# Merge gates as a stage of their own, and a recurrent state carried by a diagonal product, in a hybrid RWKV-7 and RG-LRU layer

## The chip, the cores and the metric

One Trainium2 chip, one of its cores. The metric is device microseconds of one execution; a median over runs is given where a kernel ran several times.

## The reference

One layer over 512 latent tokens behind 256 context tokens, D_MODEL 1024, fp32: half a SwiGLU FFN, two token mixers side by side on one normalised input (RWKV-7 with 16 heads of 64 in both directions, and an RG-LRU), merge gates, one output projection, and another half FFN. Cut to what this change touches:

```python
def rwkv_step(s, inp):
    r, w, k, v, kk, kka = inp
    sa = jnp.einsum('bhvk,bhk->bhv', s, -kk)
    s = s * w[:, :, None, :] + sa[..., None] * kka[:, :, None, :] + v[..., None] * k[:, :, None, :]
    y = jnp.einsum('bhvk,bhk->bhv', s, r)
    return s, y
```

The gates are two further column blocks of the input projection, 1024 columns each; a sigmoid of one scales the RWKV branch's projection, a sigmoid of the other the RG-LRU's, and the two are added.

## The kernel before

Features lie on the partitions. An fp32 product runs as three products of split operands (hi with hi, hi with lo, lo with hi: `dense`, L197 to L199), so 128 output features of 512 tokens are a column of 24 matmuls. A weight arrives by a DMA on SP's queue (L170) and is split by two instructions, hi (L161) and lo (L179), on ACT and DVE in the FFNs and on POOL in most of the input projection.

The stages are: the first FFN (to about 640 us); the input projection, eight units j of 128 features each; the recurrent stage `rwkv_phase`; the merge, the output projection and the second FFN (from about 2027 us). In the input projection each unit makes its keys, the RG-LRU's gates, then `merge_gates(j)` (two columns, a tanh on ACT, and a DMA to grw_d and glru_d), decays, reads, values and the scans; nearly all that the next stage needs goes through DRAM.

The recurrent stage has 16 units, eight pairs of heads by two directions, of 12 chunks of 64 tokens. Per unit it

- loads bk, ar and pc (`loads`), and makes the chunk Gram matrices (`gram`, 64x64 products, masks on ACT and DVE);
- inverts the triangular ones (`invert`: 31 steps of two DVE instructions, L830 and L832) and brings the result back through two DMAs, with a merge of the blocks on TensorE (`merge`, L870 and L884);
- transposes values and decays keys on TensorE (`fetch`), the latter by a diagonal matrix dg = eye * pc that POOL makes;
- walks through the 12 positions (`chain`). A position has the hops right (w = products of values and of the state s), solve (u = Y w) and step (the new state). w and u are copied out of PSUM by ACT (L941). The new state is s * pc plus two products, vt with bt and u with bt, by one DVE instruction (L984); the first state is a memset (L949).

One iteration is 24 hops, six positions of each of two units, whose chains are interleaved with a half-unit's offset: unit i is in its second half while unit i + 1 is in its first. The right side, u and the state's sum of one chain lie in one PSUM bank, ch0 or ch1 by direction.

The order of all this is written by hand: `iteration(i)` puts each operation at a hop (the table WIN), and the program is emitted in that order on all engines. Between the chain's hops lie the gram of unit i + 3, the inversion (DVE), the merge and fetch of unit i + 2, the layer norm of a finished pair (`finish`) and pieces of the filler: the RG-LRU's projection w_plru, 128 pieces of three matmuls (L1084 to L1086) whose inputs are ylru tiles (split at L202 and L203) and whose weights POOL and ACT split. In the prologue of this stage 48 pieces stand before and after the inversion of unit 0; unit 1 is inverted and merged in iteration -1, beside the first half of unit 0's chain.

Of the kernel before, what the change touches and what calls it, by code (L numbers as in the profile page):

```python
# [56 lines left out]
def hybrid_layer_kernel(ctx: ExitStack, tc, xT, vecs, cst_in, w_mod, wg1, wu1, wd1, w_in, w_up, a_up, g_up,  # L57
# [80 lines left out]
    def open_hn(st, n):  # L138
        p = st.enter_context(tc.tile_pool(name=f"hn{n}", bufs=1, reuse_waits="tile"))
# [292 lines left out]
    def input_phase():  # L432
        with ExitStack() as st:
# [257 lines left out]
            for j in range(KT):  # L691
# [4 lines left out]
                merge_gates(j)  # L696
# [15 lines left out]
    def rwkv_phase(outer):  # L712
        with ExitStack() as st:
            open_psum(st, "ps_rwkv")
            rp = outer.enter_context(tc.tile_pool(name="rwkv", bufs=1, reuse_waits="tile"))
            units = ExitStack()
            up = units.enter_context(tc.tile_pool(name="units", bufs=1, reuse_waits="tile"))
            work = lambda: bank("wk", 3)
# [13 lines left out]
            def t768(tag, bufs):  # L732
                return up.tile([128, NT], F32, tag=tag, name=tag, bufs=bufs)

            def t512(tag, bufs):
                return rp.tile([128, XT], F32, tag=tag, name=tag, bufs=bufs)
# [156 lines left out]
            def fetch(i):  # L893
                u = us[i]

                def decays():
                    j, d = divmod(i, 2)
                    u["v"] = t768("vs", 2)
                    nc.sync.dma_start(out=u["v"], in_=(zv_d, zvr_d)[d][j])
                    u["dg"] = up.tile([128, NCH, C], F32, tag="dg", name="dg", bufs=1)  # L900
                    G.tensor_tensor(out=u["dg"], in0=eye2.unsqueeze(1).to_broadcast([128, NCH, C]),
                                    in1=u["pc"].unsqueeze(2).to_broadcast([128, NCH, C]), op=ALU.mult)
                    u["bt"] = up.tile([128, NCH, 2, C], F32, tag="bt", name="bt", bufs=3)
                    u["vt"] = up.tile([128, NCH, C], F32, tag="vt", name="vt", bufs=3)
# [22 lines left out]
            def chain(i):  # L927
# [8 lines left out]
                def state():  # L936
                    return up.tile([128, C], F32, tag=f"s{d}", name="s", bufs=2)

# [63 lines left out]
            def finish(j):  # L1002
# [13 lines left out]
                def var():  # L1016
# [4 lines left out]
                    m = rp.tile([128, 12], F32, tag="rqm", name="rqm", bufs=1)[:, :8]  # L1021
                    V.tensor_scalar(out=m, in0=acc[:, :8], scalar1=1.0 / 64, scalar2=LN_EPS, op0=ALU.mult, op1=ALU.add)
                    r = rsqrt(m, 8, rp)
# [21 lines left out]
            def filler():  # L1045
# [3 lines left out]
                HX = XT // 2  # L1049

                def raw(src, c, p):
                    def go():
                        t = x["raw", c, p] = rp.tile([128, 512], F32, tag="fraw", name="fraw", bufs=2)
# [122 lines left out]
            def prologue():  # L1176
                def now(ops):
                    for op in ops:
                        op()
# [205 lines left out]
```

## Time and profile before

| | |
|---|---|
| median of 3 runs | 2550.93 us (2542.09 to 2554.51) |
| profiled execution | 2539.91 us, span 2538.1 us |
| TensorE's matmuls, busy | 2178.6 us, 86% of the span |
| VectorE | 1331.0 us, 52% |
| ScalarE | 879.5 us, 35% |
| GpSimd | 384.5 us, 15% |
[...]
| chain that ended last | PE 36%, DVE 13%, DMA 9%, issue 3%, ACT 3% |

A matmul's end is modelled, and one may overlap the next, so the distance between starts tells more than the duration. An idle time is put down to what ended it. PE is TensorE, DVE VectorE, ACT ScalarE, POOL GpSimd and SP the engine whose queue issues the DMAs.

### The profile page before, as it was taken

The numbers are of one execution on the slowest core, as the hardware profiler recorded it, in microseconds if no ns is written. First come the engines' busy times: TensorE is split into PE (matmuls) and PEld (weight loads), VectorE is DVE, ScalarE is ACT, GpSimd is POOL, SyncE is SP. The second block draws the span as 40 slices with busy tenths as digits, with TensorE's granted clock in tenths as the row PEclk, the third lists the DMA queues.
The fourth block names the chain that finished last, engine by engine and source line by source line (L and its number), as shares of the span: only waits on it lengthen the run. The fifth ranks groups of instructions, "written<-read, shape, count | busy, mean of one in ns | idle before, by whom it ended". The sixth has DMA issues, their size and how long they took to land.

```text
span 2538.1 us, 48576 instructions
## 1 busy us (share of the span) xinstructions
PE 2178.6 (86%) x19840; PEld 1832.7 (72%) x19840; DVE 1331.0 (52%) x2955; ACT 879.5 (35%) x1769; POOL 384.5 (15%) x336
## 2 busy tenths in 40 slices
PE   5999999999797989979853687578878799999997
PEld 3787878788686768767643677567777578888886
DVE  5332232235864867757654565467776356333335
ACT  5222212224554556445541232233333234322223
POOL 1000000000643434434311110011111000000000
PEclk8999999999898989989977688699999789999999
DMA  7515241223336564456663443335543352233233
GB/s 279 195 54 187 65 168 63 88 71 100 123 84 123 132 130 107 106 128 134 117 134 95 102 118 94 92 82 125 131 111 77 118 173 91 86 106 92 89 93 92
DMA packets 254655, 289.06 MB, mean 114 GB/s; under 512 B 153952, under 2 KB 172640, under 8 KB 250208
## 3 DMA queue, kind: packets, MB, share of 16 engines
q1 hardware_dynamic: 252128, 283.34, 41.2%
q10 hardware_dynamic: 2304, 2.62, 0.6%
q8 instruction: 155, 2.54, 0.4%
q14 instruction: 68, 0.56, 0.1%
HBM read 229.96 MB, written 55.93 MB: 113 GB/s over the span
## 4 chain that ended last, share of the span: by engine, by line
PE 36%; DVE 13%; DMA 9%; issue 3%; ACT 3%; SPq 1%; POOL 0%; ACTq 0%; DVEq 0%; POOLq 0%
PE mm L197 8%; PE mm L198 7%; PE mm L199 7%; PE wk L760 5%; PE ch L760 4%; DVE pr L830 2%; DMA ga_d<-sh 2%; DVE yl L832 2%; DMA y<-yt 2%; PE y L966 1%; DMA ar<-ar_d 1%; DVE s L984 1%; SPq L854 1%; PE wk L870 1%; DMA graw<-in_lru_wx_dram 1%
## 5 line engine op out<-in xcount | busy, mean ns | idle before, releaser
L197 PE MATMUL mm<-hnh,whi 128*128 128x512 f32 (+1 forms) x1896 | 672.2, 356 | 27.3 <-ACT gr L475 20.3
L198 PE MATMUL mm<-hnl,whi 128*128 128x512 f32 (+1 forms) x1896 | 670.4, 354 | 2.5 <-POOL hnl L203 1.8
L199 PE MATMUL mm<-hnh,wlo 128*128 128x512 f32 (+1 forms) x1896 | 666.9, 352 | 0.0
L197 PEld LDWEIGHTS mm<-hnh,whi 128*128 128x128 f32 x1896 | 365.3, 193 | 94.1 <-issue 38.2
L198 PEld LDWEIGHTS mm<-hnl,whi 128*128 128x128 f32 x1896 | 365.7, 193 | 58.6 <-issue 7.4
L199 PEld LDWEIGHTS mm<-hnh,wlo 128*128 128x128 f32 x1896 | 365.3, 193 | 48.0
L161 ACT ACTIVATE whi<-wraw 128x512 fp32r<-128x512 f32 (+3 forms) x264 | 193.9, 736 | 594.2 <-PE mm L198 492.5
L179 DVE TENSOR_TENSOR wlo<-wraw,whi 128x512 fp32r<-128x512 f32 (+3 forms) x264 | 216.1, 819 | 302.5 <-ACT whi L161 298.9
L197 PE MATMUL mm<-hh,whi 128*128 128x256 f32 (+1 forms) x592 | 201.4, 341 | 0.4 <-ACT hh L202 0.4
L198 PE MATMUL mm<-hl,whi 128*128 128x256 f32 (+1 forms) x592 | 201.1, 340 | 0.3 <-DVE hl L203 0.3
L199 PE MATMUL mm<-hh,wlo 128*128 128x256 f32 (+1 forms) x592 | 201.0, 340 | 0.0
L179 POOL TENSOR_TENSOR wlo<-wraw,whi 128x512 fp32r<-128x512 f32 x118 | 173.7, 1478 | 6.2
L161 POOL CAST whi<-wraw 128x512 fp32r<-128x512 f32 x118 | 101.3, 859 | 330.8 <-PE mm L198 254.9
L319 DVE TENSOR_TENSOR hf<-mm,sl 128x256 f32<-128x256 f32 (+1 forms) x68 | 40.1, 590 | 211.9 <-PE mm L199 210.0
L830 DVE TENSOR_TENSOR pr<-yl,wl 96x126 f32<-96x126 f32 (+22 forms) x496 | 140.6, 283 | 16.3 <-DMA wl<-nd 5.2
L203 POOL TENSOR_TENSOR hnl<-nt,hnh 128x256 fp32r<-128x256 f32 (+1 forms) x28 | 27.3, 976 | 796.3 <-ACT hnh L202 649.0
L832 DVE TENSOR_TENSOR yl<-yl,pr 96x126 f32<-96x126 f32 (+22 forms) x496 | 137.5, 277 | 17.1
L760 PE MATMUL wk<-ar,bk 64*64 64x128 f32 (+1 forms) x1536 | 103.7, 292 | 32.6 <-DMA ar<-ar_d 30.1
L197 PEld LDWEIGHTS mm<-hh,whi 128*128 128x128 f32 x592 | 113.0, 191 | 15.4 <-issue 1.7
L199 PEld LDWEIGHTS mm<-hh,wlo 128*128 128x128 f32 x592 | 112.9, 191 | 15.5 <-issue 2.5
L198 PEld LDWEIGHTS mm<-hl,whi 128*128 128x128 f32 x592 | 112.9, 191 | 14.3 <-issue 0.8
L760 PEld LDWEIGHTS wk<-ar,bk 64*64 64x64 f32 x1536 | 90.0, 164 | 38.8 <-issue 36.1
(239 smaller groups left out, 3414.8 us busy)
## 6 DMA issues: line engine op xcount, KB each, us to landing
wm<-in_w_mod_dram SPq DMA_DIRECT2D x32, 1024.0 KB
wraw<-in_w_in_dram SPq DMA_DIRECT2D x118, 256.0 KB
wraw<-in_wd_dram SPq DMA_DIRECT2D x64, 256.0 KB
bk_d<-bk SPq DMA_DIRECT2D x16, 768.0 KB
bk<-bk_d SPq DMA_DIRECT2D x15, 768.0 KB
wraw<-in_wg_dram SPq DMA_DIRECT2D x44, 256.0 KB
wraw<-in_wu_dram SPq DMA_DIRECT2D x44, 256.0 KB
wraw<-in_wg_dram SPq DMA_DIRECT2D x22, 512.0 KB
```

Of the source, the lines that this page charges most:

```text
L161: self.copy = (lambda o, i: eng.tensor_copy(o, i)) if eng else (lambda o, i: S.activation(o, i, AF.Copy))
L179: self.sub.tensor_tensor(out=l[:, :m], in0=raw[:, :m], in1=h[:, :m], op=ALU.subtract)
L197: PE.matmul(acc, lhsT=wh, rhs=xh, start=k == 0, stop=False)
L198: PE.matmul(acc, lhsT=wh, rhs=xl, start=False, stop=False)
L199: cur["pe"] = PE.matmul(acc, lhsT=wl, rhs=xh, start=False, stop=k == n - 1).ins.name
L203: eng.tensor_tensor(out=lo, in0=src, in1=hi, op=ALU.subtract)
L319: V.tensor_tensor(out=hf[:, :n], in0=pu[:, :n], in1=sl[:, :n], op=ALU.mult)
L760: PE.matmul(out[hp[h]], lhsT=lhsT[hp[h]], rhs=rhs[hp[h]], start=start, stop=stop)
L830: V.tensor_tensor(out=pr[:, :ni, :nt], in0=yl[:, :ni, t:t + 1].to_broadcast([96, ni, nt]), in1=wl[:, t:t + 1, t + 1:].to_broadcast([96, ni ...
L832: V.tensor_tensor(out=yl[:, :ni, t + 1:], in0=yl[:, :ni, t + 1:], in1=pr[:, :ni, :nt], op=ALU.subtract)
L854: nc.sync.dma_start(out=Y[p0:p0 + 32, :, 32 * b:32 * b + 32], in_=yd[m0:m0 + 12].rearrange("m s t -> s m t"))
L870: PE.matmul(acc[hi:hi + 32, 32 * c:32 * c + 32], lhsT=u["n"][lo:lo + 32, c, 32:64], rhs=u["y1"][lo:lo + 32, c, :].rearrange("p (q i) -> p ...
```

## The change

1. `merge_gates` leaves the input projection. Its 16 columns become `gate_columns`, the prologue of the recurrent stage: the columns follow one another on TensorE, the two grams and merges of units 0 and 1 stand between them, and both inversions are put beside them on DVE. The weights are split by ACT and DVE instead of POOL; the accumulators are the banks ch0 and ch1.
2. The pools of the normalised input and of its weights stay open until then, on the right side of SBUF, and what the chains fetch is opened in their place afterwards (vs has one buffer, was two; dg three, was one).
3. The state is no longer made by DVE: the pair dg with s is added in PSUM to the two other products, and ACT copies the sum. The products vt with bt and dg with s are issued in `solve`, behind the copy of u. The first position has no product with the state, and no memset.
4. All 128 pieces of the filler lie in the iterations: 6 in each of iterations -1 to 12 (before, 5 or fewer), some 15 in each of the last three; its ylru tiles are loaded four ahead, and those of the second half are split one after each piece of the first half's last block.

```diff
-            def merge_gates(j):
-                for col, dst in ((COL_MRW + j, grw_d), (COL_MLRU + j, glru_d)):
-                    w = wp.load(w_in[col], KT)
-                    acc = mm()
-                    dense(acc, w, hn_pairs(CT, XT))
-                    sg = t512("sg", 1)
-                    table(sg, acc, AF.Tanh, scale=0.5)
-                    nc.sync.dma_start(out=dst[j], in_=sg)
...
                 def right(pos):
                     def go():
                         c = seq[pos]
-                        if pos == 0:
-                            u["s"] = state()
-                            V.memset(u["s"], 0.0)
                         chb = u["chb"] = bank(f"ch{d}", 1)
-                        each_head(chb[:, 0:C], u["gm"][:, c], u["vt"][:, c], stop=False)
-                        each_head(chb[:, 0:C], a_of(u, c), u["s"], start=False)
+                        each_head(chb[:, 0:C], u["gm"][:, c], u["vt"][:, c], stop=pos == 0)
+                        if pos:
+                            each_head(chb[:, 0:C], a_of(u, c), u["s"], start=False)
                         u["w"] = copied(chb[:, 0:C], "w")
...
                 def solve(pos):
                     def go():
+                        c = seq[pos]
                         acc = u["chb"][:, 2 * C:3 * C]
-                        each_head(acc, u["Y"][:, seq[pos]], u["w"])
+                        each_head(acc, u["Y"][:, c], u["w"])
                         u["u"] = copied(acc, "u")
+                        if pos < last:
+                            acc = u["chb"][:, C:2 * C]
+                            each_head(acc, u["bt"][:, c, 1], u["vt"][:, c], stop=False)
+                            if pos:
+                                each_head(acc, u["dg"][:, c], u["s"], start=False, stop=False)
...
                 def step(pos):
...
-                            each_head(acc, u["bt"][:, c, 1], u["vt"][:, c], stop=False)
                             each_head(acc, u["bt"][:, c, 0], u["u"], start=False)
-                            nxt = state()
-                            V.scalar_tensor_tensor(out=nxt, in0=u["s"], scalar=u["pc"][:, c:c + 1], in1=acc, op0=ALU.mult, op1=ALU.add)
-                            u["s"] = nxt
+                            u["s"] = copied(acc, "s")
...
+                def load(n):
+                    if n < 2 * KT:
+                        q, k = divmod(n, KT)
+                        x["y", n] = rp.tile([128, HX], F32, tag="fr", name="fr", bufs=4)
+                        nc.sync.dma_start(out=x["y", n], in_=ylru_d[k, :, HX * q:HX * q + HX])
+                def mixed(n):
...
+                    split(*x["a", n], x.pop(("y", n)))
+                    load(n + 4)
...
+                        if q == 0 and m == KT - 1:
+                            mixed(KT + k)
...
+            def gate_columns():
...
+                def part(n):
+                    if n < len(cols):
+                        x["w", n] = []
+                        for t in x.pop(("raw", n)):
+                            h, l = [wpool.tile([128, 512], F32R, tag=f"w{w}", name=f"w{w}", bufs=WB[1]) for w in ("hi", "lo")]
+                            split(h, l, t)
+                            x["w", n].append((h, l))
+                def column(n):
...
+                        part(n + 1)
+                        load(n + 2)
+                        w = x.pop(("w", n))
+                        acc = bank(("ch0", "ch1")[n % 2], 1)
+                        dense(acc, lambda k: [t[:, 128 * (k % 4):128 * (k % 4) + 128] for t in w[k // 4]], hn_pairs(CT, XT))
+                        sg = wpool.tile([128, XT], F32, tag="sg", name="sg", bufs=1)
+                        S.activation(sg, acc, AF.Tanh, scale=0.5)
+                        nc.sync.dma_start(out=cols[n][1], in_=sg)
...
+                for i in range(3):
+                    beside(0, 1, loads(i))
+                first(0, 1)
+                first(1, 3)
+                inverse(0, 3, 8)
+                inverse(1, 8, 13)
+                beside(9, 10, [lambda: [op() for op in merge(0)]])
+                beside(14, 15, [lambda: [op() for op in merge(1)]])
```

What moves is seen in the order of the instructions. First TensorE at two positions of the interleaved chains, before: the solves (w with Y, here ybd) of both chains stand one behind the other, then the products of the state. A number behind ch or ybd tells one buffer from another, a bracket the engine whose instruction a row waits for.

```order
L760 MATMUL ch_15537<-w,ybd_10913 64x64 [waits Activation_49]
L760 MATMUL ch_15537<-w,ybd_10913 64x64
L760 MATMUL ch_15544<-w,ybd_10917 64x64 [waits Activation_49]
L760 MATMUL ch_15544<-w,ybd_10917 64x64
L760 MATMUL ch_15537<-vt,bt 64x64 [waits Activation_49]
L760 MATMUL ch_15537<-vt,bt 64x64
L760 MATMUL ch_15537<-u,bt 64x64 x2
L760 MATMUL ch_15544<-vt,bt 64x64 [waits Activation_49]
L760 MATMUL ch_15544<-vt,bt 64x64
L760 MATMUL ch_15544<-u,bt 64x64 x2
L988 MATMUL y<-gm,u 64x64 x2
L760 MATMUL wk<-dg,bk 64x64 x16
```

The same place after the change:

```order
L756 MATMUL ch_12053<-w,ybd_10268 64x64 [waits Activation_49]
L756 MATMUL ch_12053<-w,ybd_10268 64x64
L756 MATMUL ch_12053<-vt,bt 64x64 [waits Activation_49]
L756 MATMUL ch_12053<-vt,bt 64x64
L756 MATMUL ch_12053<-s,dg 64x64 x2
L756 MATMUL ch_12060<-w,ybd_10270 64x64 x2
L756 MATMUL ch_12060<-vt,bt 64x64 [waits Activation_49]
L756 MATMUL ch_12060<-vt,bt 64x64
L756 MATMUL ch_12060<-s,dg 64x64 x2
L756 MATMUL ch_12053<-u,bt 64x64 x2
L982 MATMUL y<-gm,u 64x64 x2
L756 MATMUL ch_12060<-u,bt 64x64 x2
```

The products vt with bt (and the new s with dg) have moved up to stand between the two solves, and the first of each pair waits for ACT, where u is copied; the second chain's solve stands behind it.

Second, SP's queue at the end of the input projection, before: the last RG-LRU result ylru_d is followed by the loads of units 0 to 2 (bk and ar of unit 0 are on ACT's queue here), the Gram matrices' way through DRAM (nd, wl), and then values and filler.

```order
L683 DMA ylru_d<-gr 128x512
L751 DMA pc<-pc_d 128x12
L745 DMA bk<-bk_d 128x1536
L747 DMA ar<-ar_d 128x1280
L751 DMA pc<-pc_d 128x12
L745 DMA bk<-bk_d 128x1536
L747 DMA ar<-ar_d 128x1280
L751 DMA pc<-pc_d 128x12
L810 DMA nd<-gm 32x12x32 x4
L814 DMA wl<-nd 48x1024 x2
L899 DMA vs<-zv_d 128x768
L1071 DMA fr<-ylru_d 128x256 x8
```

And after the change:

```order
L673 DMA ylru_d<-gr 128x512
L1135 DMA grw_d<-sg 128x512
L741 DMA bk<-bk_d 128x1536
L743 DMA ar<-ar_d 128x1280
L747 DMA pc<-pc_d 128x12
L741 DMA bk<-bk_d 128x1536
L743 DMA ar<-ar_d 128x1280
L747 DMA pc<-pc_d 128x12
L741 DMA bk<-bk_d 128x1536
L743 DMA ar<-ar_d 128x1280
L747 DMA pc<-pc_d 128x12
L1112 DMA wraw<-in_w_in_dram 128x512 x2
```

The first gate's result (grw_d) stands ahead of the loads of units 0 to 2, all of which are on SP now, and the weights of a further column behind them.

## Rows read from the trace of the kernel before

**Rows 1.** Stages: length; busy of PE, PEld, DVE, ACT, POOL; clock; DMA share, GB/s.

```profile
728.00:1318.00 590.00, 504.76 (x2391) 402.49 (x2389) 396.77 (x547) 303.86 (x464) 234.11 (x201) 0.91 0.57 117
1318.00:1407.00 89.00, 33.53 (x432) 31.53 (x432) 29.30 (x88) 13.44 (x28) 13.49 (x11) 0.71 0.46 136
1407.00:1458.00 51.00, 36.44 (x628) 32.79 (x628) 33.70 (x118) 12.87 (x33) 9.55 (x8) 0.70 0.38 100
1458.00:1949.00 491.00, 377.99 (x8918) 345.25 (x8918) 320.72 (x1161) 144.86 (x504) 54.96 (x43) 0.89 0.43 105
```

**Rows 2.** TensorE's waits, 680 to 1310 us: total, times, longest.

```profile
PE mm L199 <- DVE glo L179: 29.2, 5, 10.4
```

**Rows 3.** TensorE's waits, 1420 to 2010 us.

```profile
PE ch L760 <- DVE s L984: 65.7, 45, 15.0
PE wk L870 <- DMA y<-yt: 26.6, 11, 3.6
PE ch L760 <- DVE s L949: 18.4, 14, 2.2
PE ch L760 <- ACT u L941: 18.2, 37, 1.2
```

**Rows 4.** Timeline of DVE, then of PE, prologue: start, duration, what, [idle before, releaser].

```profile
1317.74 0.69 DVE L682 TENSOR_TENSOR gr<-gr,gel 128x512 f32<-128x512 f32 x1
...
1422.38 0.28 DVE L984 SCALAR_TENSOR_TENSOR s<-s,pc,ch 128x64 f32<-128x64 f32 x1 [1.39 <-PE ch L760]
...
1327.94 8.79 PE L760 MATMUL wk<-ar,bk 64*64 64x64 f32 x160 [30.11 <-DMA ar<-ar_d]
...
1348.39 1.12 PE L760 MATMUL wk<-eye,vs 64*64 64x64 f32 x16 [7.17 <-DMA vs<-zv_d]
```

**Rows 5.** Timeline of all engines, one position of the last chain.

```profile
2002.10 0.33 PE L760 MATMUL ch<-w,ybd 64*64 64x64 f32 x4 [0.15 <-ACT w L941]
2002.54 0.22 ACT L941 ACTIVATE u<-ch 128x64 f32<-128x64 f32 x1 [0.49 <-PE ch L760]
...
2002.82 0.33 PE L760 MATMUL ch<-vt,bt 64*64 64x64 f32 x4 [0.38 <-ACT u L941]
...
2003.37 0.28 DVE L984 SCALAR_TENSOR_TENSOR s<-s,pc,ch 128x64 f32<-128x64 f32 x1 [2.15 <-PE ch L760]
...
2003.70 0.33 PE L760 MATMUL ch<-vt,gm 64*64 64x64 f32 x4 [0.32 <-DVE s L984]
```

**Rows 6.** Timeline of SP's queue, gates of unit 0.

```profile
728.34 0.33 SPq L626 DMA_DIRECT2D grw_d<-sg  x1
...
733.83 0.33 SPq L626 DMA_DIRECT2D glru_d<-sg  x1
```

**Rows 7.** The page's costliest groups: DVE's weight remainders.

```profile
L179 DVE TENSOR_TENSOR wlo<-wraw,whi 128x512 fp32r<-128x512 f32 (+3 forms) x264 | 216.1, 819 | 302.5 <-ACT whi L161 298.9
```

**Rows 8.** Timeline of PE at 1840 us, both levels of the clock.

```profile
1840.37 0.42 PE L966 MATMUL y<-gm,vt 64*64 64x64 f32 x4
1840.58 0.42 PE L966 MATMUL y<-ar,s 64*64 64x64 f32 x4
...
1843.53 0.28 PE L1084 MATMUL fl<-fx,fhi 128*128 128x256 f32 x1
1843.64 0.28 PE L1085 MATMUL fl<-fx,fhi 128*128 128x256 f32 x1
...
1844.37 0.28 PE L760 MATMUL ch<-vt,bt 64*64 64x64 f32 x4
1844.49 0.28 PE L760 MATMUL ch<-u,bt 64*64 64x64 f32 x4
```

**Rows 9.** Timeline of PE at the two long stalls.

```profile
1593.37 0.48 PE L760 MATMUL ch<-vt,gm 64*64 64x64 f32 x4 [11.90 <-DVE s L984]
...
1644.97 0.48 PE L760 MATMUL ch<-vt,gm 64*64 64x64 f32 x4 [15.03 <-DVE s L984]
```

More of the change, by code (lines that the diff above doesn't have):

```diff
@@ L1076, in piece, with raw @@
-                def piece(c, k, src, dst):
-                    def go():
+                rp = late["rp"]
+                flat = [(q, m, p) for q in range(2) for m in range(KT) for p in range(2)]
+                def raw(n):
+                    if n < len(flat):
+                        q, m, p = flat[n]
+                        t = x["raw", n] = rp.tile([128, 512], F32, tag="fraw", name="fraw", bufs=2)
+                        nc.sync.dma_start(out=t, in_=w_plru[m][:, 512 * p:512 * p + 512])
@@ new lines, in mixed, with piece @@
+                def mixed(n):
+                    k = n % KT
+                    x["a", n] = [rp.tile([128, HX], F32R, tag=f"fx{w}{k}", name=f"fx{w}{k}", bufs=1) for w in range(2)]
+                    split(*x["a", n], x.pop(("y", n)))
+                    load(n + 4)
+                def piece(n, k):
+                    def go():
+                        q, m, p = flat[n]
+                        if k == 0 and n == 0:
+                            raw(0)
+                            for y in range(4):
+                                load(y)
+                            raw(1)
+                            weights(0)
+                            for y in range(KT):
+                                mixed(y)
+                        if k == 4 * p:
+                            raw(n + 2)
+                            weights(n + 1)
@@ L1111, in filler, with load, go @@
-                return ops
+                return [piece(n, k) for n, (q, m, p) in enumerate(flat) for k in range(4 * p, 4 * p + 4)]
+            def gate_columns():
+                cols = [(COL_MRW + j, grw_d[j]) for j in range(KT)] + [(COL_MLRU + j, glru_d[j]) for j in range(KT)]
+                x = {}
+                def load(n):
+                    if n < len(cols):
+                        x["raw", n] = [wpool.tile([128, 512], F32, tag="wraw", name="wraw", bufs=WB[0]) for _ in range(2)]
+                        for p, t in enumerate(x["raw", n]):
+                            nc.sync.dma_start(out=t, in_=w_in[cols[n][0]][:, 512 * p:512 * p + 512])
+                def part(n):
+                    if n < len(cols):
+                        x["w", n] = []
[4 more added lines that the diff above has]
+                def column(n):
+                    def go():
+                        if n == 0:
+                            load(0)
+                            part(0)
+                            load(1)
+                        part(n + 1)
[6 more added lines that the diff above has]
+                        nc.sync.dma_start(out=cols[n][1], in_=sg)
+                    return go
+                return [column(n) for n in range(len(cols))]
@@ L1176, in prologue @@
             def prologue():
-                def now(ops):
-                    for op in ops:
-                        op()
-                def feed(n):
-                    now(fill[:n])
-                    del fill[:n]
-                for i in range(3):
-                    now(loads(i, nc.sync if i else nc.scalar))
-                for i in range(2):
-                    ops, out = gram(i)
-                    now(ops)
-                    out(QS[i])
-                now(fetch(0))
-                feed(PRO[0])
@@ L1193, in prologue, with beside, first @@
-                ops, back = invert(0)
-                now(ops)
-                back()
-                feed(PRO[1])
-                now(merge(0))
-                put(-1, [(-0.9, unit_invert(1, HOPS + 17.0, (HOPS, HOPS + 15.0)))])
+                gate = gate_columns()
+                todo = {n: [op] for n, op in enumerate(gate)}
+                def beside(a, b, ops):
+                    for at, op in spread(ops, a, b):
+                        todo[int(at)].append(op)
+                def first(i, at):
+                    ops, out = gram(i)
+                    beside(at, at + 1, ops[:3] + [out])
+                    beside(at + 1, at + 2, ops[3:])
@@ new lines, in inverse, with go @@
+                def inverse(i, a, b):
+                    def go():
+                        ops, back = invert(i)
+                        for op in ops[:n]:
+                            op()
+                        rest[i] = ops[n:], back
+                    n = 2
+                    rest = {}
+                    beside(a, a + 1, [go])
+                    for q in range(a + 1, b):
+                        def go(q=q):
+                            ops, back = rest[i]
+                            k = -(-len(ops) // (b - q))
+                            for op in ops[:k]:
+                                op()
+                            rest[i] = ops[k:], back
+                            if q == b - 1:
+                                back()
+                        beside(q, q + 1, [go])
```

113 lines of the change are left out of this document (41 added, 72 removed).

## The prediction

> **What bounds the kernel now.** I read the table by stage first. In the input projection TensorE works 504.8 us of 590, and in the recurrent stage 378.0 of 491 at a granted clock of 0.89; only in the prologue between them (89 us) is it busy for 33.5 us, at 0.71 [rows 1]. So TensorE is the engine to price, and an edit is worth what it does to TensorE's own work or to its idle time. The waits of TensorE come next: the longest of the input projection is on DVE's weight remainder, 29.2 us in 5 places [rows 2]; in the recurrent stage it waits for the state of DVE (65.7 us, 45 times), for a transposed inverse on its way through a DMA (26.6, 11), for the copy of u (18.2, 37) and for the memset of a state (18.4, 14) [rows 3]. Last I read single positions of the chain and the first chain step on the timeline [rows 4, 5].
>
> **The change part by part.** The sum is made against the profiled execution, 2539.9 us. That one is 0.4% below the median of the runs shown (2550.9), so what I forecast is the median plus the sum.
>
> *Gates out of the input projection.* The two results of a unit leave 5.49 us apart (728.34 and 733.83) [rows 6], which is one column of 24 matmuls. Sixteen of them are 88 us. Against that, the first two columns of the new stage have their four weight remainders on DVE inside the last unit, 0.82 us each [rows 7], 3 us. I take -85. The other bound: DVE and ACT follow TensorE closely in that stage (DVE 396.8 us of 590 [rows 1]) and the 29.2 us wait for DVE [rows 2] shows that TensorE can be held by it; were half of the gates' time only cover for DVE, -45 would be left. I choose the upper end because TensorE's idle time there, 85 of 590, is small beside the work. The weight splits that POOL did go with the gates, and POOL is busy 234 of 590 us [rows 1]: it gates nothing, so nothing is gained there.
>
> *Prologue.* Before, the last DVE instruction of the input projection starts at 1317.74 and the first state at 1422.38: 104.6 us, 30.1 of them TensorE's wait for ar [rows 4]. After, the queue order puts ar's load where it was, about 10 us behind that DVE instruction; two columns run before it lands, in time that is idle now, and 14 come behind it: 77 us. Two grams (most of their matmuls are one run of 8.8 us at the low clock [rows 4], so 11 for the two) and two merges, by estimate 6, stand between the columns. The inversions of units 0 and 1, DVE work, lie beside the columns, and the cover holds: a column needs 1.6 us of DVE for its two remainders [rows 7] and leaves 4 of its 5.5. With 7 us of hand-overs the columns end some 111 us after that mark. Then vs is loaded, values and keys are transposed and the first hops follow. Before, 74 us lie between the end of TensorE's wait for vs at 1348.39 and the first state [rows 4], most of it filler, inversion and merge; without these I allow 21, with another wait for vs of about 7 in it. That is about 132, which is 28 later. The 48 pieces of the filler that stood in the prologue are gone from it; this is counted in the 132. The first chain iteration, 51 us with DVE busy for 33.7 [rows 1], loses unit 1's inversion and merge: I take 9 off. Net **+19**, bounds +8 (the columns cover the loads wholly) and +35 (each column waits a little for its weights, whose buffers stay three).
>
> *The solve.* Here the order is what counts. Now both chains solve, back to back or with filler behind them, and then comes the first product with bt; it waits for u's copy, since it writes the bank that ACT reads, but much of the copy has passed. In the change each solve is followed at once by the products of that same bank, and these carry the wait on ACT. The second chain's solve, the filler and the y products stand behind the waiting instruction on TensorE's queue. One such trip is on the timeline where nothing covers it: solve 2002.10, copy 2002.54, next product 2002.82 [rows 5]: 0.72 us, of which 0.12 is the solve's own issue [rows 8] and 0.60 is lost. There are 16 units of 11 such positions, 176: 106 us, of which 18.2 are paid already [rows 3]. **+88**. From below: a trip whose copy starts at once cannot be much shorter than 0.6 in issue time, so 0.45 each, +61; from above, ACT may be in a 0.6 us instruction when u is ready (half of the 176 times, 0.3 us more), +114.
>
> *The products dg·s.* 16 units of 10 positions, each one pair of small matmuls at 0.12 (1844.37 to 1844.49) [rows 8]: **+19**.
>
> *Filler.* 48 pieces move from the prologue into the iterations, three 256-column matmuls each, 0.11 to 0.12 apart (1843.53 to 1843.64) [rows 8], 0.35 a piece: **+17**. Nothing covers them now, since the fill stands behind the new wait.
>
> *The state.* A state costs DVE 0.28 us and a copy costs ACT 0.22 [rows 5]. From copy to use: the DVE state begins 2003.37, right begins 2003.70, and TensorE idles 0.32 of it [rows 5]. The 45 waits include two of 11.9 and 15.0 [rows 9], so the others are 38.8 in 43, 0.9 each: most is DVE's queue (the inversion's steps), not the instruction. ACT is busy 145 us of 491 and DVE 321 [rows 1]; with 39 us of copies ACT is still the emptier. I take **-15**, bounds 0 (ACT's copies queue behind its evictions) and -38. [...]
>
> *The memset* of the first state is gone, with the 18.4 us that TensorE waits there, behind DVE's queue [rows 3]: **-18**.
>
> *The inverse's DMA.* The merge keeps its hop. Hops now take longer by more than the mean wait, 26.6 in 11 or 2.4 us, so the DMA is mostly covered: **-24**, bounds -5 and -26.
>
> *The two long stalls.* ACT stands for half of ylru until its DMA lands, the state waits behind it, and TensorE idles 11.9 and 15.0 us [rows 9]. The change loads four such tiles ahead and splits one for each piece: **-27**, bounds -10 and -27.
>
> Sum: -85 + 19 + 88 + 19 + 17 - 15 - 18 - 24 - 27 = **-26**. On the profiled execution 2514, on the median **2525**. The final merge and both FFNs hold the same instructions; I price them at nothing.
>
> **The rivals.**
> (a) *Absorbed.* The solve's wait is at its lower bound (+61) and the state's waits go wholly (-38), because bt's and dg's products are done early and only u's pair stands before the copy; the prologue comes out at +15. That is -26 - 27 - 23 - 4 = -80: **2471**. For it: 0.9 us per state wait against 0.32 where DVE is free [rows 3, 5]. Against it: these waits are on a copy that ACT takes in program order too.
> (b) *Slower: the clock.* 176 new stops of TensorE make its clock fall. The small pair is issued in 0.21 us at the low level (1840.37 to 1840.58) and 0.12 at the high one [rows 8]. The stage's 378 busy us at 0.89 are 336 at full clock; at a granted 0.75, close to that of the prologue with its idle time [rows 1], they are 448. That adds 70: **2595**. It decides from about 0.81 downward (336/0.81 is 415, +37, then it is slower than before). For it: 0.70 and 0.71 stand exactly where TensorE idles most [rows 1]. Against it: the fill gives TensorE long runs, and gates' columns raise the prologue. [...]
> (c) *The input projection keeps the time.* DVE and ACT set the pace of a unit and the gates only filled TensorE: -50 instead of -85, **2560**, no measurable change. For it: the 29.2 us wait for DVE [rows 2]. Against it: 85% busy.
>
> **How the numbers follow.** A measurement of this kernel tells about 0.5%, 12.7 us, from no change: 2538.2 and 2563.7. The forecast case has 0.42, with its own range of 2498 to 2552; (a) 0.20, (b) 0.20, (c) 0.18. Faster: 0.31 of the forecast, all of (a), 0.02 of (c), 0.53. Same: 0.09 of the forecast, 0.09 of (c), 0.02 of (b), 0.20. The rest, 0.27, is slower: 0.02, 0.07 and 0.18. With the bounds of the solve and of the prologue at either side the range is 2465 to 2595.
>
> **What would show it.** In the profile after: columns 5.5 us apart in the new stage and an input projection 80 to 90 us shorter; the first state about 130 us after the last DVE instruction of the input projection; some 170 waits of TensorE on u, 0.6 us each, as the largest group of the recurrent stage; no waits on a memset; no wait over 5 us on ylru; waits on the state, now from ACT, under 30 us. A sum of waits on u under 60 us would speak for (a), a granted clock under 0.81 in the recurrent stage for (b), an input projection only 50 us shorter for (c).

## The result and the profile after

The change takes 2483.57 us (median of four, 2476.26 to 2496.28), the kernel before 2549.48 beside it: a ratio of 0.9749, 95% interval 0.9701 to 0.9798. That is 64 us less, where 26 were forecast and the range allowed 2465 to 2595. A second chip gave 0.9745 for the same kernel (0.97 to 0.9791).

The table by stage of the change (columns as in [rows 1]) has the input projection, the new prologue up to the first state, and the recurrent stage from the first state to the last y:

```profile
728.00:1245.00 517.00, 427.06 (x2045) 337.48 (x2044) 391.13 (x553) 292.31 (x450) 170.06 (x136) 0.91 0.62 112
1245.00:1381.00 136.00, 109.94 (x936) 90.71 (x938) 59.85 (x174) 37.81 (x75) 6.97 (x6) 0.86 0.53 157
1381.00:1953.00 572.00, 471.60 (x11084) 417.34 (x11092) 328.99 (x1095) 214.06 (x781) 75.81 (x59) 0.97 0.43 107
```

The same cuts in the kernel before, prologue and recurrent stage:

```profile
1318.00:1422.00 104.00, 44.86 (x607) 41.77 (x609) 33.59 (x102) 17.98 (x38) 19.19 (x15) 0.70 0.43 129
1422.00:2015.00 593.00, 458.54 (x10513) 414.73 (x10509) 369.19 (x1333) 171.72 (x600) 62.41 (x49) 0.88 0.40 97
```

So the input projection is 73 us shorter (590 in [rows 1]), the prologue 32 longer, and the recurrent stage 21 shorter; the rest differs by 2. The third is what a reader would not get from the work alone: the recurrent stage holds more matmuls than before (11084 records against 10513), and it is shorter. Its granted clock is 0.97, was 0.88 (0.947 and 0.918 over the whole execution). In short windows the traces show it at 0.50 or at 1.00: before, 0.50 from 1840.30 to 1841.00 us and 1.00 from 1843.50 to 1844.70 (the two spacings of [rows 8]); after, 0.50 from 1610.30 to 1611.50 and 1.00 from 1604.60 to 1606.00. If these two levels alone make up the means, that is an estimated 34 us at the lower one in the 572, where it was 142 in the 593. TensorE's waits in it, after:

```profile
PE ch L756 <- ACT u L934: 79.3, 175, 1.4
PE ch L756 <- ACT s L934: 15.6, 23, 2.4
...
PE wk L866 <- DMA y<-yt: 1.5, 2, 0.8
```

Against [rows 3]: 175 waits on u for 37, as the order of the instructions said; the waits on the state are 15.6 for 65.7; the memset's are gone; those on the transposed inverse are 1.5 for 26.6. One position pair on the timeline of PE shows the new stops, two solves each followed by its wait on ACT, and only then the filler:

```profile
1599.95 0.28 PE L756 MATMUL ch<-w,ybd 64*64 64x64 f32 x4
1600.62 0.33 PE L756 MATMUL ch<-vt,bt 64*64 64x64 f32 x4 [0.38 <-ACT u L934]
1600.79 0.28 PE L756 MATMUL ch<-s,dg 64*64 64x64 f32 x4
1600.90 0.28 PE L756 MATMUL ch<-w,ybd 64*64 64x64 f32 x4
1601.57 0.33 PE L756 MATMUL ch<-vt,bt 64*64 64x64 f32 x4 [0.38 <-ACT u L934]
1601.73 0.28 PE L756 MATMUL ch<-s,dg 64*64 64x64 f32 x4
1601.95 0.38 PE L1090 MATMUL fl<-fx,fhi 128*128 128x256 f32 x1
```

From solve to the next product 0.67 us, 0.12 of it the solve's own issue: 0.55 lost, twice a pair. The list of waits counts only the idle part of such a stop, 0.38 here and 0.45 on average, since the solve's modelled end comes 0.28 us after its start.

In the input projection the waits of TensorE grew a little; the chain of ACT, DVE and the RG-LRU's weights now seems to stand bare in places:

```profile
PE mm L197 <- ACT gr L475: 30.0, 4, 10.2
PE mm L199 <- DVE glo L179: 29.4, 4, 11.3
PE mm L197 <- ACT ghi L161: 19.4, 6, 7.6
```

The remainder's wait is as in [rows 2]; ACT's gr and ghi were 20.3 and 13.7 before:

```profile
PE mm L197 <- ACT gr L475: 20.3, 4, 8.9
PE mm L197 <- ACT ghi L161: 13.7, 4, 4.7
```

In the prologue TensorE still waits for ar (30.1 in [rows 4]), and the state that the first chain step needs comes 136 us after the last ylru_d is sent; two rows of PE and ACT:

```profile
1255.70 5.39 PE L756 MATMUL wk<-ar,bk 64*64 64x64 f32 x64 [17.95 <-DMA ar<-ar_d]
1380.64 0.20 ACT L934 ACTIVATE s<-ch 128x64 f32<-128x64 f32 x1
```

### The profile page after: what moved, and what is told of

The parts are those of the page before. It is cut to its first block, busy times and chain, and to the rows that moved or that the text cites. A ratio compares the mean times of both kernels' runs of the same rounds, so it can differ in the third digit from the quotient of the medians.

```text
span 2474.5 us, 49715 instructions
## 1 busy us (share of the span) xinstructions
PE 2174.4 (88%) x20408; PEld 1817.1 (73%) x20416; DVE 1312.9 (53%) x2795; ACT 935.0 (38%) x1977; POOL 323.0 (13%) x272
## 4 chain that ended last, share of the span: by engine, by line
PE 38%; DMA 4%; ACT 4%; DVE 4%; issue 3%; SPq 1%; POOL 0%; ACTq 0%; POOLq 0%; DVEq 0%
PE ch L756 7%; PE mm L198 6%; PE mm L197 6%; PE mm L199 6%; PE wk L756 6%; ACT u L934 2%; PE y L957 1%; PE fl L1090 1%; DMA yraw<-yrw_d 1%; DMA ga_d<-sh 1%; PE wk L880 1%; PE fl L1091 1%; PE fl L1092 1%; PE wk L866 1%; PE ch L197 1%
## 5 line engine op out<-in xcount | busy, mean ns | idle before, releaser
L197 PE MATMUL mm<-hnh,whi 128*128 128x512 f32 (+1 forms) x1768 | 620.1, 352 | 37.0 <-ACT gr L475 30.0
L198 PE MATMUL mm<-hnl,whi 128*128 128x512 f32 (+1 forms) x1768 | 618.5, 350 | 2.8 <-POOL hnl L203 1.9
L199 PE MATMUL mm<-hnh,wlo 128*128 128x512 f32 (+1 forms) x1768 | 615.3, 348 | 0.0
L197 PEld LDWEIGHTS mm<-hnh,whi 128*128 128x128 f32 x1768 | 339.7, 193 | 98.1 <-issue 47.2
L198 PEld LDWEIGHTS mm<-hnl,whi 128*128 128x128 f32 x1768 | 339.9, 192 | 53.4 <-issue 7.4
L199 PEld LDWEIGHTS mm<-hnh,wlo 128*128 128x128 f32 x1768 | 339.6, 192 | 42.4
L179 POOL TENSOR_TENSOR wlo<-wraw,whi 128x512 fp32r<-128x512 f32 x86 | 131.2, 1526 | 6.1
L756 PE MATMUL ch<-vt,bt 64*64 64x64 f32 x704 | 59.3, 246 | 79.7 <-ACT u L934 79.7
L161 POOL CAST whi<-wraw 128x512 fp32r<-128x512 f32 x86 | 80.3, 935 | 305.2 <-PE mm L198 234.5
L343 DVE SCALAR_TENSOR_TENSOR res<-mm,scl,res 128x256 f32<-128x256 f32 (+1 forms) x112 | 66.8, 597 | 92.9 <-PE mm L199 92.1
```

What stands on the lines that cost most here:

```text
L161: self.copy = (lambda o, i: eng.tensor_copy(o, i)) if eng else (lambda o, i: S.activation(o, i, AF.Copy))
L179: self.sub.tensor_tensor(out=l[:, :m], in0=raw[:, :m], in1=h[:, :m], op=ALU.subtract)
L197: PE.matmul(acc, lhsT=wh, rhs=xh, start=k == 0, stop=False)
L198: PE.matmul(acc, lhsT=wh, rhs=xl, start=False, stop=False)
L199: cur["pe"] = PE.matmul(acc, lhsT=wl, rhs=xh, start=False, stop=k == n - 1).ins.name
L343: V.scalar_tensor_tensor(out=res[:, m, q:q + n], in0=acc[:, :n], scalar=scl[:, gi, m, v:v + 1], in1=res[:, m, q:q + n], op0=ALU.mult, op1= ...
```

## The experiments

Each row of the table is a run of its own; ratios are to the kernel before on the same chip, and the stage is from the first state to the last y. Waits are TensorE's, in us.

| run | ratio (95%) | stage | u | state + memset | inverse (y) | clock |
|---|---|---|---|---|---|---|
| before | 1 | 592 | 18 | 66 + 18 | 27 | 0.88 |
| the change | 0.9749 (0.9701 to 0.9798) | 572 | 79 | 16 | 2 | 0.97 |
| the change again | 0.9745 (0.97 to 0.9791) | 572 | 80 | 16 | 0 | 0.96 |
| products in step | 0.9619 (0.959 to 0.9648) | 542 | 15 | 12 | 46 | 0.92 |
| state on DVE | 0.9698 (0.9663 to 0.9732) | 558 | 15 | 35 + 17 | 32 | 0.92 |
| state part alone | 1.0011 (0.9979 to 1.0043) | 605 | 79 | 37 | 10 | 0.91 |
| loads ahead alone | 0.987 (0.984 to 0.99) | 568 | 19 | 36 + 18 | 36 | 0.90 |
| in step, inversion early | 0.9644 (0.9616 to 0.9672) | 549 | 29 | 12 | 7 | 0.93 |
| on DVE, inversion early | 0.9828 (0.9796 to 0.9859) | 600 | 15 | 84 + 25 | 0 | 0.89 |
| way back late | 0.9759 (0.9729 to 0.9789) | 584 | 80 | 16 | 5 | 0.95 |
| in step, loads after | 0.9486 (0.945 to 0.9522) | 513 | 16 | 10 | 6 | 0.94 |
| the same, y1 first | 0.948 (0.9453 to 0.9508) | 508 | 17 | 10 | 0 | 0.95 |
| on DVE, loads after | 0.9668 (0.9639 to 0.9696) | 556 | 15 | 49 + 18 | 3 | 0.90 |
| fastest, gates in the input | 0.9675 (0.9652 to 0.9698) | 509 | 20 | 9 | 15 | 0.95 |

**Products in step.** The change, with the two early products moved:

```diff
                 def solve(pos):
...
-                        if pos < last:
-                            acc = u["chb"][:, C:2 * C]
-                            each_head(acc, u["bt"][:, c, 1], u["vt"][:, c], stop=False)
-                            if pos:
-                                each_head(acc, u["dg"][:, c], u["s"], start=False, stop=False)
                 def step(pos):
...
                             acc = u["chb"][:, C:2 * C]
+                            each_head(acc, u["bt"][:, c, 1], u["vt"][:, c], stop=False)
+                            if pos:
+                                each_head(acc, u["dg"][:, c], u["s"], start=False, stop=False)
```

> The change, but the products vt with bt and dg with s are issued in step again, behind both solves and the filler, ahead of u with bt; ACT still copies the state. Theory (stops on u): the 175 stops on u, 79 us of idle time, fall to about 20 us because the second solve and the filler cover the copy, and the time falls by 45 to 65 us against the change, to about 2430. Rival (the chain's length is what counts): the state's sum now has two pairs of products more between u and its copy, the waits on the state rise by what the waits on u lose, and the time stays within 12 us of the change.

The waits on u fall from 79 to 15 us as expected, and the waits on the state don't rise, so the rival falls. But by the ratios only 33 us are gained (30 in the stage), not 45 to 65: the inverse is late again.

```profile
PE wk L866 <- DMA y<-yt: 46.3, 12, 7.0
PE ch L756 <- ACT u L934: 15.0, 29, 0.7
PE ch L756 <- ACT s L934: 12.2, 23, 2.3
```

And the clock is lower, 0.92. The timeline of PE around one such stop shows both levels: small pairs start 0.12 us apart ahead of it, 0.21 behind it, and 0.12 again after 1619.

```profile
1608.35 0.28 PE L756 MATMUL ch<-s,dg 64*64 64x64 f32 x4
1608.46 0.28 PE L756 MATMUL ch<-u,bt 64*64 64x64 f32 x4
1608.58 0.28 PE L980 MATMUL y<-gm,u 64*64 64x64 f32 x4
1612.37 1.65 PE L866 MATMUL wk<-y,gm 32*32 32x32 f32 x48 [3.50 <-DMA y<-yt]
...
1614.43 0.42 PE L756 MATMUL ch<-vt,gm 64*64 64x64 f32 x4
1614.64 0.42 PE L756 MATMUL ch<-s,ar 64*64 64x64 f32 x4
1614.85 0.42 PE L957 MATMUL y<-gm,vt 64*64 64x64 f32 x4
...
1619.19 0.28 PE L756 MATMUL ch<-s,dg 64*64 64x64 f32 x4
1619.30 0.28 PE L756 MATMUL ch<-u,bt 64*64 64x64 f32 x4
```

**State on DVE.** The change, with memset, DVE's instruction, and both products of the old state in step.

```diff
-                            u["s"] = copied(acc, "s")
+                            nxt = state()
+                            V.scalar_tensor_tensor(out=nxt, in0=u["s"], scalar=u["pc"][:, c:c + 1], in1=acc, op0=ALU.mult, op1=ALU.add)
+                            u["s"] = nxt
```

> The change, but with the state as before: memset, one DVE instruction per state, no product with dg, both products with bt in step. Theory (stops on u cost what they show): waits on u back to about 20 us, dg's 19 us of work gone, against that waits on the state up by 20 to 40 and on the memset up by 18; the sum is a time within 20 us of the change, so that the gain of the change is not this part's. Rival (the state on ACT is the gain): the state's waits and the lower clock come back and it is 30 us or more slower than the change.

The ratio is 0.9698, half a per cent below the change's 0.9749, but the two intervals overlap, so the two are not told apart. The theory (within 20 us) holds and the rival falls: this part, in the form that the change gives it, shows no gain. What it saves in waits on the state, the memset and the inverse (84 us with the state on DVE, 17 in the change), it spends on u (15 and 79) and on dg's product (19 by the price in the prediction).

**State part alone.** The kernel before, with right, solve and step of the change and its numbers of buffers (vs 1, dg 3).

```diff
-                    u["dg"] = up.tile([128, NCH, C], F32, tag="dg", name="dg", bufs=1)
+                    u["dg"] = up.tile([128, NCH, C], F32, tag="dg", name="dg", bufs=3)
-                            V.scalar_tensor_tensor(out=nxt, in0=u["s"], scalar=u["pc"][:, c:c + 1], in1=acc, op0=ALU.mult, op1=ALU.add)
+                            u["s"] = copied(acc, "s")
```

> The kernel before with the state's part of the change alone (dg product, ACT's copy, vt with bt in solve, no memset; buffers of vs and dg as in the change). Theory: waits on u +60 us, dg +19, memset -18, state -10 to -40, transposed inverse -24: between -10 and +30 against the kernel before, both stalls on ylru still there. Rival (this part is the gain, by way of the clock): 25 us or more faster than before, with a granted clock of 0.95 or more in the recurrent stage outside the two stalls.

No difference (1.0011), inside the theory's range, and the rival falls. TensorE's waits have those on u of the change, and the two stalls inside those on the state (11.6 and 12.1):

```profile
PE ch L760 <- ACT u L938: 78.9, 175, 1.3
PE ch L760 <- ACT s L938: 36.8, 25, 12.1
PE wk L870 <- DMA y<-yt: 10.2, 2, 9.7
```

**Loads ahead alone.** The kernel before with the filler of the change (`load`, `mixed`, `piece`).

```diff
-                            x["y", k] = rp.tile([128, HX], F32, tag="fr", name="fr", bufs=3)
+                        x["y", n] = rp.tile([128, HX], F32, tag="fr", name="fr", bufs=4)
...
+                    split(*x["a", n], x.pop(("y", n)))
+                    load(n + 4)
```

> The kernel before with the filler's new loads alone: ylru tiles four ahead, second half split one tile after each piece; 48 operations in the prologue as before, now all of them pieces. Theory: the two stalls of 11.9 and 15.0 us go, 25 to 30 us faster than before, and the granted clock between 1576 and 1674 us rises from 0.71 and 0.83 to that of the iterations beside. Rival: the stall only moves to the next wait (the state behind ACT's splits, the transposed inverse), and less than 12 us are gained.

1.3% or 33 us faster by the ratios, a little above the theory's 25 to 30, so the rival falls. In the profiled executions, which are of different chips (2538 and 2525 us in all), the recurrent stage is 24 us shorter (568 for 592); 3 of them, by the price of a piece in the prediction, are nine pieces of the filler that lie in the prologue instead. No wait on ylru is left in the stage, while those on the inverse grow from 27 to 36 us. Around the stalls the clock was 0.71 and 0.83 before (the first two rows), and it is 0.93 in a window there now:

```profile
1576.00:1623.00 47.00, 30.57 (x657) 27.40 (x653) 23.29 (x85) 13.07 (x44) 2.61 (x2) 0.71 0.35 83
1623.00:1674.00 51.00, 28.61 (x692) 26.47 (x690) 26.77 (x99) 11.09 (x39) 3.79 (x3) 0.83 0.33 87
...
1580.00:1680.00 100.00, 80.52 (x1955) 74.14 (x1955) 67.72 (x244) 30.48 (x108) 12.96 (x10) 0.93 0.48 117
```

**The change again; the inversion earlier; the way back later.** Three runs beside a repetition of the change.

> The change once more, unaltered, as the base for the runs beside it on this chip. Every theory expects 0.970 to 0.980 of the kernel before, and about 175 waits on u of 79 us together.

The earlier inversion is an edit of the table of hops, made to the run with the products in step and to the one with the state on DVE:

```diff
-            WIN = dict(fin=(0.6, 4.6, 8.6, 16.6), gram=(0.7, 3.4, 4.7, 16.7, 20.7), out=5.0, inv=(11.0, 32.0), back=34.0,
+            WIN = dict(fin=(0.6, 4.6, 8.6, 16.6), gram=(0.7, 3.4, 4.7, 16.7, 20.7), out=5.0, inv=(10.5, 28.0), back=30.0,
```

> The change with vt with bt and dg with s in step, as in the first run of that edit, and with the inversion four hops shorter and its way back through DRAM four hops earlier (hops 10.5 to 28 and 30, were 11 to 32 and 34). Theory (the 46 us of waits for the transposed inverse were what ate the gain, and they lowered the clock): these waits fall below 15 us, the granted clock of the recurrent stage rises from 0.92 to 0.96 or more, and the time falls by 35 to 60 us against the change without these edits, about 0.955 of the kernel before. Rival (the DMA's own length bounds the merge, or the queue of SP does, whatever the hop): the wait stays over 30 us and the time within 10 us of that first run, 0.962.

> The same earlier inversion, but with the state as before the change (memset, DVE's instruction, no dg product). Theory: the waits for the transposed inverse (32 us) go here too, those on DVE's state (35) and on the memset (17) stay or grow, because the denser inversion shares DVE with the state: 10 to 30 us slower than the run beside it with ACT's copies. Rival (the state on DVE is the better one, since dg's product costs 19 us of TensorE): as fast or faster than that run.

With ACT's copies the wait for the inverse falls from 46 to 7 us, but nothing is won: 0.9644, where the products in step alone had 0.9619. DVE's masks behind the denser inversion now hold TensorE up (12.1, 6.6 and 5.7 us on gm, waits that the run before it does not have), and u's waits double (28.8 us for 15.0). On DVE the waits on the state grow (84 us, 35 without the earlier inversion), and this run is 1.9% or 50 us slower than its neighbour. The theory of the second run held in its direction, not in its size of 10 to 30 us; that of the first held for the wait only. The edit does two things: four hops earlier, the reads also stand ahead of the loads of unit i + 4 on SP's queue, so this run doesn't say which of the two took the wait for the inverse away.

The way back alone, in the change:

```diff
-            WIN = dict(fin=(0.6, 4.6, 8.6, 16.6), gram=(0.7, 3.4, 4.7, 16.7, 20.7), out=5.0, inv=(11.0, 32.0), back=34.0,
+            WIN = dict(fin=(0.6, 4.6, 8.6, 16.6), gram=(0.7, 3.4, 4.7, 16.7, 20.7), out=5.0, inv=(11.0, 32.0), back=38.0,
```

> The change, with the inverse's way back through DRAM four hops later (38, was 34), so that TensorE has one long stop per unit at the merge. Theory (a few long stops lower the granted clock, 175 short ones do not): about 14 stops of 4 to 7 us, the granted clock of the recurrent stage falls from 0.97 to 0.93 or less, and the time rises by more than the stops: 75 us of stops and 15 to 30 us by the clock. Rival (the clock follows the total idle time or the work, not the length of a stop): the clock stays at 0.96 or above and the time rises by the stops alone.

This run doesn't tell the theories apart, because the edit didn't make the stops: TensorE waits 4.5 us in 3 places and not 75 in 14, and the time is that of the change (0.9759 and 0.9745). On SP's queue the reads stand behind the same loads as in the change, and they go out 6.6 us after yt is written, where in the same unit of the change it is 6.1 (written at 1590.92, read back at 1597.03):

```profile
1603.55 1.66 SPq L840 DMA_DIRECT2D yt<-ylt  x2
1605.26 0.58 SPq L741 DMA_DIRECT2D bk<-bk_d  x1
1605.88 0.47 SPq L743 DMA_DIRECT2D ar<-ar_d  x1
...
1610.17 3.37 SPq L853 DMA_DIRECT2D y<-yt  x2
```

**Loads after, and the transposed inverse first.** In the run with the products in step, SP's queue shows what the inverse stands behind: yt is written at 1635.62, and only behind the loads of unit i + 4 and the four blocks is it read back, at 1645.32. These 9.7 us are the longest of the 16 units; the median is 6.9.

```profile
1635.62 2.52 SPq L840 DMA_DIRECT2D yt<-ylt  x2
...
1639.35 0.37 SPq L741 DMA_DIRECT2D bk<-bk_d  x1
1639.82 0.38 SPq L743 DMA_DIRECT2D ar<-ar_d  x1
1640.25 0.42 SPq L747 DMA_DIRECT2D pc<-pc_d  x1
1640.76 4.52 SPq L850 DMA_DIRECT2D ybd<-yd  x4
1645.32 3.23 SPq L853 DMA_DIRECT2D y<-yt  x2
```

```diff
-                    put(i, [(9.1, op) for op in loads(i + 4)])
+                    put(i, [(10.6, op) for op in loads(i + 4)])
```

> The change with vt with bt and dg with s in step, and with the loads of unit i + 4 (bk, ar, pc) on SP's queue behind the inverse's reads instead of ahead of them (hop 10.6, was 9.1). Theory (the inverse arrives late because 1.4 MB of loads stand ahead of it, and the long stops this makes also lower the clock): the waits for the transposed inverse fall from 46 us to 15 or less, the granted clock of the recurrent stage rises from 0.92 to 0.95 or more, and the recurrent stage is 30 us or more shorter than with that edit alone (542): about 0.95 of the kernel before. Rival (the way through DRAM takes that long by itself): the waits stay above 35 us, and the time at 0.96.

The waits for the inverse are 5.5 us, the stage 513 (542), the ratio 0.9486: the theory holds, though the clock came to 0.94 and not 0.95. The second edit turns round the two groups of reads in `back`, y1 ahead of Y:

```diff
                     Y = u["Y"] = ybd[i % 3]
+                    u["y1"] = up.tile([128, NCH, 32], F32, tag="y1", name="y1", bufs=1)
+                    for h in range(2):
+                        nc.sync.dma_start(out=u["y1"][64 * h:64 * h + 32],
+                                          in_=yt[12 * h:12 * h + 12].rearrange("m t q i -> t m (q i)"))
                     for b in range(2):
...
-                    u["y1"] = up.tile([128, NCH, 32], F32, tag="y1", name="y1", bufs=1)
-                    for h in range(2):
-                        nc.sync.dma_start(out=u["y1"][64 * h:64 * h + 32],
-                                          in_=yt[12 * h:12 * h + 12].rearrange("m t q i -> t m (q i)"))
```

> As the run before it, and the transposed inverse, which the merge reads first, is read back ahead of the four blocks that it reads second. Theory: it lands about 4 us earlier, and no stop of over 2 us is left at the merge; the granted clock reaches that of the change, 0.96, and the time is 0.94 to 0.95 of the kernel before. Rival (the second read is then late by as much): the wait moves to the merge's second half, and the time is that of the run before it.

Now yt is read back 5.1 us after it is written (the median of the units is 4.7), and the four blocks and the loads stand behind it:

```profile
1584.92 1.65 SPq L840 DMA_DIRECT2D yt<-ylt  x2
1590.01 0.84 SPq L848 DMA_DIRECT2D y<-yt  x2
1591.02 3.03 SPq L854 DMA_DIRECT2D ybd<-yd  x4
1594.09 0.47 SPq L1096 DMA_DIRECT2D plru_d<-sg  x1
1594.60 0.43 SPq L741 DMA_DIRECT2D bk<-bk_d  x1
```

No wait for it is left in the list, nor one of the merge's second half for its blocks (the 2.8 us in 2 places that TensorE idles before it are put down to nothing that the profile shows), so the rival's cause falls; but the loads are late in turn (ar, 11.8 us in 7), and the time is that of the run before it:

```profile
PE ch L756 <- ACT u L934: 16.5, 29, 1.7
PE wk L756 <- DMA ar<-ar_d: 11.8, 7, 3.3
PE ch L756 <- ACT s L934: 10.4, 22, 1.0
```

At 2425.46 us, 0.948, it is the fastest kernel here, level with the run before it, and its ratio is 0.027 below that of the change.

The same place of the loads with DVE's state is one edit more of the second run above:

```diff
-                    put(i, [(9.1, op) for op in loads(i + 4)])
+                    put(i, [(10.6, op) for op in loads(i + 4)])
```

> The same later loads, but the state as before the change (memset, DVE's instruction, no dg product). Theory (DVE's queue holds the state up): the waits on the state and the memset stay near 52 us, the clock stays below 0.95, and it is 0.5% or more slower than the run with ACT's copies. Rival (dg's 19 us and the copies cost as much as they save): within 0.5% of it.

0.9668 against 0.9486: with the other waits out of the way, ACT's copies are worth 1.8%. The theory holds; TensorE waits 49 us for the state from DVE's queue and 18 for the memset, 67 together and more than the 52 expected.

**The gates in the input projection.** The kernel before with all of the fastest run but the gates' stage: gates in the units, the old prologue with 48 pieces of the filler, unit 1 inverted in iteration -1. Against the fastest run, cut to its core:

```diff
                 u.keys()
                 l.gates()
+                merge_gates(j)
                 l.decays()
...
-                gate = gate_columns()
-                todo = {n: [op] for n, op in enumerate(gate)}
...
+                feed(PRO[0])
+                ops, back = invert(0)
+                now(ops)
+                back()
+                feed(PRO[1])
+                now(merge(0))
```

> The fastest run so far without the gates' stage: the kernel before, with the gates in the input projection, the prologue and unit 1's inversion in iteration -1 as before, and everything else of that run (state by dg's product in step, ACT's copy, ylru tiles loaded ahead, loads behind the inverse's reads, transposed inverse first). Theory (the input projection gives 74 us, the prologue takes 32 back, the filler that leaves the prologue takes some 14): 20 to 45 us slower than that run, 0.956 to 0.966 of the kernel before. Rival (the gates only filled idle time in the input projection): within 10 us of it.

0.9675 against 0.948, 50 us: the gates' stage, with the order of the prologue that goes with it, is a gain of its own, a little above the theory's 20 to 45. The rival falls. Its recurrent stage is as long as the fastest run's (509 and 508), although it holds fewer pieces of the filler and one more inversion and merge, so the gain lies ahead of it: the last ylru_d is sent at 1325.7 us (1253.1 in the fastest run), and the first state comes 112.5 us later (141.2), which makes 44 in the profiled executions.

## Why the prediction was right, and where its sizes were off

The direction and the range held; the range is 130 us wide, and the forecast was 38 us short. Of the signs named ahead, the first state, the count of the waits on u, the memset, ylru and the state came as said; the input projection is 73 us shorter and not 80 to 90.

- *Gates out of the input projection*, -85: measured -73. The difference is about that of the waits on ACT (gr and ghi, 15 us more in sum); no run separates it. Rival (c), -50, is refuted by the stage's length and by the last run.
- *Prologue*, +28 to the first state: measured +32. The columns mostly follow one another at 5.4 to 6.0 us where no gram or merge stands between them, as priced, but two columns covered the wait for ar only in part (17.9 are left of 30.1).
- *The solve*, +88: the trip was priced at 0.60 and is 0.55, and the count, 176, was right at 175. That is 96 us, less the 18.2 paid before, an estimated +78. The list of waits gives 61 (79.3 less 18.2), the lower bound that rival (a) took, but it counts the idle part of each trip alone.
- *The state*, -15, with the two stalls, -27: together -50 (65.7 or 65.9 to 15.6). The stalls are gone whole. The other waits were 38.8, of which the forecast left 24 to ACT's queue; 15.6 are left. The term was too small by some 8 us.
- *The memset and the inverse*, -18 and -24: -18 and -25, as priced.
- *dg and filler*, +19 and +17: the filler's term was mis-sized by a count. The 48 operations of the prologue held 9 that load and split ylru, so 39 pieces moved, an estimated 14 us.
- *The clock* had no term in the forecast, and rival (b) had it fall. It rose, from 0.88 to 0.97, and this is the step that failed: a term put at nothing. Its size stays open. All waits of the stage sum to 31 us less (133 and 102), and 24 us of work came in by the corrected terms (19, 14, less 9 for the first iteration), which would leave 7 of gain; 20 were measured. So some 13 us are left for the clock, or 30 if the solve is taken at 78 and not at 61. By the reckoning of rival (b), the busy time before is 404 us of work at full clock (458.5 at 0.88), which at 0.97 take 416, 43 us less; that is an upper bound, since busy time goes by modelled ends. These are estimates, 13 to 43 us, and no run separates the clock from the rest.

Rival (a) came nearest in its number, 2471, and mostly by luck: outside the stalls the waits on the state fell from 38.8 to 15.6 and not to nothing, the prologue came out longer than it had it, and it had no term for the clock either. The waits on u did not get absorbed; they are there, 175 of them, and moving the products takes 64 us of them out again.

The runs put the parts of the change at: ylru's loads ahead about -1.3%, the gates' stage about -2% (in the fastest form; the change itself was not run without it), the state's part nothing by itself and nothing that can be told from noise inside the change. The first two make -3.3% against the change's -2.5%; the remainder is hardly above the noise. So, as far as runs of single parts tell, the 21 us of the recurrent stage go with ylru's loads (24 shorter with them alone), not with the state's part (605 us with it alone, 592 before). The state's part is a good idea in the wrong place: with the two products behind both solves and the filler, and the inverse's reads ahead of the bulk loads, the same part is worth 1.8%.

## What to carry to other kernels

Here a product that goes into the bank which an eviction is reading stopped not only itself but all that stood behind it on TensorE, 0.55 us each time: issue such a product after the work that can cover the eviction, even if its operands are ready long before. When such a stop is removed, look at once for the transfer that had been hidden by it; here it was a small read that stood behind 1.4 MB of loads on one queue. Turning the two round gained 1.3% (0.9619 to 0.9486); starting the computation earlier, which put the read ahead of the loads as well, gained nothing, because other waits grew. A part that measures nothing alone may be held up by a wait that another edit removes, so try it again after that edit.

## What the runs showed of the hardware

Stops of TensorE of half a microsecond, 175 of them in 572 us, went with a granted clock of 0.96 to 0.97 in the change; in the run with the products in step, 12 waits that sum to 46 us, the longest 7.0, went with 0.92, though all its waits together are shorter (85 us against 102). Behind a stop of 3.5 us in that run the small pairs start 0.21 us apart, the lower level, and later 0.12 again. So in these two runs the lower clock went with the longer stops (7.0 us at most, against 2.4 in the change), not with the many of half a microsecond. It is a correlation over these runs: the run that was to set it by itself did not make the stops it was meant to make (4.5 us in 3 places, clock 0.95), and that stays open.
